# First projection reordered around its input loads, with six small moves in the second half of a two-layer decoder kernel

## The chip, the cores and the metric

One Trainium2 chip; the program runs on one of its cores. The metric is the device time of one execution in microseconds (us), the median of several runs. The core has a matrix engine (TensorE, PE in the profile, with its weight loads listed as PEld), a vector engine (VectorE, DVE), an activation engine (ScalarE, ACT), a general engine (GpSimd, POOL) and a queue engine that mostly issues DMA transfers (SyncE, SP). POOL can issue DMA transfers too. Each engine runs its own instructions strictly in the order in which they stand, and waits on semaphores where it needs another engine's or a transfer's result.

## The reference, cut to what matters

A trunk of two layers over 512 tokens of width 1024, all in float32. Layer 0 has dilated window attention, layer 1 attention with a forget gate over shared keys and values ("FoX"); each layer ends in a gated feed-forward part with a causal convolution of width 3.

```python
def dilated_mixer(xn, w_qkv, w_o, cos, sin):
    qkv = xn @ w_qkv                       # first projection: (512, 1024) x (1024, 2304)
    ...
def fox_mixer(xn, w_q, w_o, k, v, c):
    q = (xn @ w_q).reshape(B, T, B_HEADS, HEAD_DIM)
    for i in range(T // BLK):              # blocks of 128 queries, causal key prefixes
        s = einsum('bqhd,bkhd->bhqk', q_i, k[:, :q1]) * scale + (c_q - c_k)
        p = softmax(where(causal, s, NEG))
        outs.append(einsum('bhqk,bkhd->bqhd', p, v[:, :q1]))
    return concat(outs) @ w_o              # output projection: (512, 1024) x (1024, 1024)
def conv_ffn(xn, w_up, cw, cb, w_down):
    a = conv3(xn @ w_up) + cb
    gate, val = split(a, 2)
    return (gelu(gate) * val) @ w_down     # (512, 2816) x (2816, 1024)
def reference(...):
    for l in range(2):
        h = h + rms_norm(mix_l(rms_norm(h, g[0])), g[1])
        h = h + rms_norm(conv_ffn(rms_norm(h, g[2]), ...), g[3])
```

## The kernel before, in words

**Numbers.** Each float32 operand is cut into a high part in a shorter format and the rest, the low part; a product is then three matmuls: high by high, low by high, high by low. For weights, `Weights.high` (L55) makes the high part on ACT (L60), and `Weights.low` (L65) the low part on DVE (L69). A weight piece is 512 KB, named `wraw` (`wearly` for the first six) until it is cut, and `w` after that. `Weights.load` (L47) issues the transfers on SP's queue. `W.get()` hands out the next piece and cuts ahead as far as `W.ahead` says.

**Order.** The kernel is recorded with its own order (L221): instructions stand on each engine as the Python code emits them. Buffers come from pools (16 of 8 KB a partition, `t8`; 10 of 4 KB, `t4`; 8 of 2 KB, `t2`; 8 PSUM banks), and an instruction that takes a buffer waits until its last user has finished.

**First projection (L1251 to L1339).** The input x is loaded in half blocks: block b of 128 tokens, half i of 512 columns, `load_x(b, i)`, 256 KB each, from SP (L228). `transpose0` (L1257) turns four 128x128 squares of a half block on PE into PSUM (`xt_ps`), `split0` (L1266) makes the scaled high part on ACT (`xah`, L1271) and the low part on DVE (`xal`, L1273). `qk0(b, s)` (L1279) multiplies block b with weight piece s: two column groups k, three matmuls each, six matmuls of 128x512 (L1290) into `qk_ps`, which accumulates over four pieces. Before all this PE runs matmuls on a zeroed tile (`warm_up`, L243; `WARM = 4, 5`): four ahead of the first transposes, five behind them. The first real work needs the gains (`g0_rows`), half block (0, 0) and piece 0.

**FoX (L1840 to L1901).** A loop over m = 0 to 17; each m below 16 is a pair (j, i0) with j a pair of heads and i0 = 0 or 2, for two query blocks i0 and i0 + 1. In step m PE makes the scores of pair m (`s_ps`, L1759), the value products of pair m - 2 (`o_ps`, L1806), and then, in two half steps a = 0 and 1, a quarter of the next query projection (`q_ps`) and the transposes of the probabilities of pair m - 1 (`pT_ps`, L1791). POOL makes the bias one step ahead (L1740, L1741), DVE the maximum and the sum with the bias (`nm`, L1767), ACT the exponential (L1769), DVE the reciprocal and the scaling (L1777, L1779), ACT the copies of transposed probabilities (`pT`, L1793). From half step 26 on (`FILL`, m = 13) the first products of the output projection fill PE (`acc`, L277 to L279, with activations `OTb`); their weight pieces 1 to 3 are cut by `W.high()` from (j, i) = (6, 1) and `W.low()` from (6, 2) on. Piece 0 is cut earlier with an adding transfer.

**Sums of down weights.** The second-layer down projection uses sums of quarter blocks of its weights, made ahead and stored in the DRAM tile `dT`. `down_sums` (L590) is a generator that loads a pair of rows from SP, makes four DVE operations, and stores on a given queue. Inside the FoX loop `sums_between` (L1822) does the same for j = 2, 3, 4, 5: load on POOL's queue (L1827 to L1829), two DVE operations (L1831, L1832), two more (L1834, L1835), one store on POOL's queue (L1837). The table at L1854 says in which (m, half step) each part runs: with m = 2, 6, 10, 14 they are (m, 1), (m+1, 2), (m+2, 0), (m+2, 1), where half step 2 is the end of the step.

Of the kernel before, what the change touches and what calls it, by code (L numbers as in the profile page):

```python
# [9 lines left out]
F32 = mybir.dt.float32  # L10
# [8 lines left out]
KD = D // 128  # L19
# [3 lines left out]
EPS = 1e-6  # L23
# [5 lines left out]
ND = NF // 2  # L29
HALVES = (slice(0, 1024),), (slice(0, 512), slice(512, 1024))  # L30
WARM = 4, 5
LAST = 3
# [73 lines left out]
def trunk_kernel(ctx, tc, x, norm_gains, w_qkv_a, w_o_a, w_q_b, w_o_b, kv_norm, w_kvf, b_f,  # L106
# [127 lines left out]

    eps_t = cst.tile([128, 1], F32, name="eps_t")
    dve.memset(eps_t, EPS)
    g_rows = t2([8, 128], name="g0_rows")

    zero = t2([128, 512], BF16, name="zero")
    dve.memset(zero, 0.0)  # L240
    warm = bank([128, 512], name="warm")

# [347 lines left out]
    def down_sums(pairs, place, queue, lag, behind):  # L590
# [3 lines left out]
        for i in range(n + lag + behind):  # L594
# [15 lines left out]
            if i >= 0:  # L610
                l, j = pairs[i]
                for q, t in enumerate(live[i]):
                    queue.dma_start(dT[l][j, :, q * 1024:q * 1024 + 1024], t)
            yield
# [15 lines left out]
    def ffn(l, bd, cp, nxt, ahead):  # L630
# [343 lines left out]
        for c in range(2, NF):  # L974
            if c == NF - 4:
                pair_load(0)
            if c == NF - 3:
                sums = down_sums([(l, ND - 1), (1, 8 + l)], in_one, pool, 1, 0)
                next(sums)
# [277 lines left out]
    def transpose0(b, i):  # L1257
        n = 2 if (b, i) == (0, 0) else 4
        for k0 in range(0, 4, n):
            pt = bank([128, n, 128], name="xt_ps")  # L1260
            for k in range(n):
                c = (4 * i + k0 + k) * 128
                pe.transpose(pt[:, k, :], h[:, b, c:c + 128], ident)
                x_ps[b, 4 * i + k0 + k] = pt[:, k, :]
# [13 lines left out]

    def qk0(b, *pieces):  # L1279
        if b not in qk_banks:  # L1280
            qk_banks[b] = bank([128, T], name="qk_ps")
        o = qk_banks[b]
        for s in pieces:
            if s not in ws:
                ws[s] = [t.rearrange("p (k c) -> p k c", k=2) for t in W.get()]
            wh, wl = ws[s]
            for x, w in ((0, wh), (1, wh), (0, wl)):
                for k in range(2):
                    kc = 2 * s + k
                    pe.matmul(o, ax(0, b, kc)[x], w[:, k, :], start=kc == 0 and x == 0 and w is wh,  # L1290
                              stop=kc == KD - 1 and w is wl)

# [17 lines left out]
    qk0(2, 0, 1)  # L1310
    W.split(4)
# [27 lines left out]
    qk_post(0, 3, qk_banks[3])  # L1339
    sums = down_sums([(1, 6), (1, 7)], in_two, sp, 1, 3)  # L1340
    next(sums)
# [29 lines left out]

    down0 = down_sums([(0, j) for j in range(10)], in_one, sp, 1, 1)
    v_proj0([[L(qk_transpose, 0, 0), L(qk_transpose, 0, 1)],
# [448 lines left out]
    def sums_between(l, j):  # L1822
# [7 lines left out]
        yield  # L1830
        dve.tensor_tensor(a[:, 0:512], a[:, 512:1024], a[:, 0:512], ALU.subtract)  # L1831
        dve.tensor_tensor(a[:, 512:1024], b[:, 0:512], a[:, 512:1024], ALU.subtract)  # L1832
        yield
# [20 lines left out]
    for j, m in ((2, 2), (3, 6), (4, 10), (5, 14)):  # L1854
        g = sums_between(1, j)
        for i in ((m, 1), (m + 1, 2), (m + 2, 0), (m + 2, 1)):
            sums[i] = g
    for m in range(M + 2):
# [17 lines left out]
        for a in range(2):  # L1876
# [76 lines left out]
```

## Time and profile before

| what | us |
|---|---|
| median of 3 runs | 1107.63 (1106.81 to 1109.08) |
| the profiled execution's own time | 1107.05 |
| its span, first to last instruction | 1105.0 |
| PE busy | 1096.0 |
| DVE busy | 894.8 |
| ACT busy | 667.4 |
| POOL busy | 222.7 |

The profile lists for each instruction its start, its duration, and, in brackets, how long its engine stood idle before it and what ended that. The time line merges equal instructions that follow each other (x5 is five of them, with the time from the first start to the last end). Ends of matmuls are modelled and overlap the next start, so the pace of PE is read from start to start. Times in the text are counted from the start of the span. The profiled execution took 0.6 us less than the median.

### The profile page before, as it was taken

What the parts mean: (1) busy time and instruction counts of PE and PEld (TensorE: products, weight loads), DVE (VectorE), ACT (ScalarE), POOL (GpSimd) and SP (SyncE); (2) the same over time, 40 slices, a digit from 0 to 9 for tenths busy, and PEclk for the clock granted to TensorE, in tenths of its full rate; (3) what the DMA queues carried; (4) which work ended last, traced back from release to release, by engine and by line L of the source; (5) the groups of instructions that cost most, each with busy time, mean ns of one, the idle gap of its engine ahead of it and who ended that gap; (6) DMA issues with size and microseconds to landing.
All of it is one profiled execution on the core that took longest, in us unless ns stands there. A gap on an engine that the chain in (4) does not pass through costs nothing.

```text
span 1105.0 us, 18176 instructions
## 1 busy us (share of the span) xinstructions
PE 1096.0 (99%) x6608; PEld 948.5 (86%) x6608; DVE 894.8 (81%) x1510; ACT 667.4 (60%) x1120; POOL 222.7 (20%) x331
## 2 busy tenths in 40 slices
PE   9999999999999999999999999999999999999997
PEld 7988889899999988888888778789899999988886
DVE  5677778878887799997877877958978887799994
ACT  6654565656556547576565677655656566547572
POOL 4632101111111111000010766501111111111000
PEclk9999999999999999999999999999999999999999
DMA  9589854468788989894872677574468788999872
GB/s 320 109 290 407 335 151 136 112 148 191 180 194 206 278 312 341 284 321 98 210 153 77 209 229 204 160 233 134 106 146 192 176 200 210 265 314 342 292 248 77
DMA packets 185218, 237.33 MB, mean 215 GB/s; under 512 B 11872, under 2 KB 131672, under 8 KB 184616
## 3 DMA queue, kind: packets, MB, share of 16 engines
q1 hardware_dynamic: 167560, 176.61, 49.9%
q0 software_dynamic: 17568, 59.55, 23.2%
q8 instruction: 52, 0.85, 0.3%
q14 instruction: 38, 0.31, 0.1%
HBM read 170.28 MB, written 39.63 MB: 190 GB/s over the span
## 4 chain that ended last, share of the span: by engine, by line
PE 96%; ACT 2%; DVE 1%; issue 0%; DMA 0%; DVEq 0%; SPq 0%; ACTq 0%
PE up L277 13%; PE up L278 13%; PE up L279 13%; PE acc L277 8%; PE acc L278 8%; PE acc L279 8%; PE qk_ps L1290 2%; PE v_ps L277 2%; PE v_ps L278 2%; PE v_ps L279 2%; PE s_ps L1759 1%; PE o_ps L1806 1%; PE q_ps L277 1%; PE first L279 1%; PE first L277 1%; PE first L278 1%
## 5 line engine op out<-in xcount | busy, mean ns | idle before, releaser
L277 PE MATMUL acc<-w 128*128 128x512 f32 (+1 forms) x311 | 120.5, 388 | 0.0
L279 PE MATMUL acc<-w 128*128 128x512 f32 (+1 forms) x311 | 120.4, 387 | 0.0
L60 ACT CAST w<-wraw 128x1024 fp32r<-128x1024 f32 x96 | 99.0, 1049 | 9.6 <-issue 3.8
L278 PE MATMUL acc<-w 128*128 128x512 f32 (+1 forms) x267 | 103.2, 387 | 0.0
L639 ACT ACTIVATE bb<-up,conv 128x512 f32<-128x512 f32 x80 | 60.0, 776 | 67.3 <-DVE up L1020 42.8
L69 DVE TENSOR_TENSOR w<-wraw,w 128x1024 fp32r<-128x1024 f32 x66 | 88.0, 1353 | 12.9 <-ACT w L60 12.5
L278 PE MATMUL up<-xcl,w 128*128 128x512 f32 (+1 forms) x280 | 96.3, 344 | 0.0
L278 PE MATMUL up<-xbl,w 128*128 128x512 f32 (+1 forms) x280 | 96.3, 344 | 0.0
L277 PE MATMUL up<-xbh,w 128*128 128x512 f32 (+1 forms) x280 | 96.3, 344 | 0.0
L277 PE MATMUL up<-xch,w 128*128 128x512 f32 (+1 forms) x280 | 96.3, 344 | 0.0
L279 PE MATMUL up<-xbh,w 128*128 128x512 f32 (+1 forms) x280 | 96.2, 344 | 0.0
L279 PE MATMUL up<-xch,w 128*128 128x512 f32 (+1 forms) x280 | 96.2, 344 | 0.0
L277 PE MATMUL up<-xsh,w 128*128 128x256 f32 x320 | 90.6, 283 | 0.0
L278 PE MATMUL up<-xsl,w 128*128 128x256 f32 x320 | 90.6, 283 | 0.0
L279 PE MATMUL up<-xsh,w 128*128 128x256 f32 x320 | 90.6, 283 | 0.0
L279 PEld LDWEIGHTS acc<-w 128*128 128x128 f32 x311 | 58.4, 188 | 12.0
L277 PEld LDWEIGHTS acc<-w 128*128 128x128 f32 x311 | 58.4, 188 | 11.7
L642 DVE SCALAR_TENSOR_TENSOR bb<-up,conv,bb 128x510 f32<-128x510 f32 x80 | 59.9, 749 | 2.8
L640 DVE SCALAR_TENSOR_TENSOR bb<-up,conv,bb 128x511 f32<-128x511 f32 x80 | 59.4, 743 | 2.6 <-ACT bb L639 2.6
L277 PEld LDWEIGHTS up<-xsh,w 128*128 128x128 f32 x320 | 61.4, 192 | 0.0
L278 PEld LDWEIGHTS up<-xsl,w 128*128 128x128 f32 x320 | 61.4, 192 | 0.0
L279 PEld LDWEIGHTS up<-xsh,w 128*128 128x128 f32 x320 | 61.4, 192 | 0.0
(336 smaller groups left out, 3157.4 us busy)
## 6 DMA issues: line engine op xcount, KB each, us to landing
wraw<-in_w_up_dram SPq DMA_DIRECT2D x88, 512.0 KB
w<-wraw POOLq DMA_DIRECT2D x50, 512.0 KB, 5.9
dT<-dsums SPq DMA_DIRECT2D x24, 512.0 KB
hD<-hc POOLq DMA_DIRECT2D x44, 256.0 KB, 7.8
dact<-hD SPq DMA_DIRECT2D x44, 256.0 KB
wraw<-dT SPq DMA_DIRECT2D x22, 512.0 KB
wraw<-in_w_down_dram SPq DMA_DIRECT2D x22, 512.0 KB
dsums<-in_w_down_dram SPq DMA_DIRECT2D x18, 512.0 KB
```

What stands on the lines that cost most here:

```text
L60: self.nc.scalar.copy(pair[:, 0, s], raw[:, s])
L69: self.nc.vector.tensor_tensor(pair[:, 1, s], raw[:, s], pair[:, 0, s].bitcast(F32), ALU.subtract)
L277: pe.matmul(o, ah, bh, start=first, stop=False, skip_group_check=shared)
L278: pe.matmul(o, ah, bl, start=False, stop=False, skip_group_check=shared)
L279: pe.matmul(o, al, bh, start=False, stop=last, skip_group_check=shared)
L639: act.activation(bb[:, s, :], ps, AF.Identity, bias=cp[:, 3, ch:ch + 1], scale=cp[:, 2, ch:ch + 1])
L640: dve.scalar_tensor_tensor(bb[:, s, 1:], ps[:, :T - 1], cp[:, 1, ch:ch + 1], bb[:, s, 1:], ALU.mult, ALU.add)
L642: dve.scalar_tensor_tensor(bb[:, s, 2:], ps[:, :T - 2], cp[:, 0, ch:ch + 1], bb[:, s, 2:], ALU.mult, ALU.add)
L1290: pe.matmul(o, ax(0, b, kc)[x], w[:, k, :], start=kc == 0 and x == 0 and w is wh, stop=kc == KD - 1 and w is wl)
L1759: pe.matmul(s[i][hh][:, :nn], q[a][rows, qs], k[b][rows, :nn], start=n == 0, stop=n == 2)
L1806: pe.matmul(o[64 * hh:64 * hh + 64, i * 128:(i + 1) * 128], Vt[hd // 8][:, k, (hd % 8) * 64:(hd % 8) * 64 + 64], pT[j, i, hh][:, k, :], st ...
```

## The change

Line numbers behind the first edits shift by one to six; the new kernel's rows below carry its own.

- **Loads.** Piece 1 of the weights is asked for behind half blocks (1, 0) and (2, 0), not ahead of them.
- **Warm-up.** Six matmuls ahead of the first transposes and three behind them (before four and five). The zeroed tile is set ahead of the epsilon constant.
- **First projection.** `qk0` takes its matmuls in another order (high, low, high, low for the two column groups with the weight's high part, then the two with its low part) and can call a function in their midst, between the first group's and the second's. The transposes of half blocks (1, 0), (2, 0), (3, 0) go there, and the products of pieces 0 and 1 come in the order 0 for blocks 0, 1, 2, then 1 for blocks 0, 1, 2. The first-half transposes of all blocks use two PSUM banks of two squares each, and are split two at a time.
- **Stores.** `down_sums` takes a list of queues; the second store of `down1` goes to SP and not to POOL.
- **Sums.** `sums_between` has five parts: the first of its DVE operations runs half a step earlier, in (m+1, 1).
- **Output weights.** `W.high()` from (6, 0) and `W.low()` from (6, 1), half a step earlier each.

```diff
-WARM = 4, 5
+WARM = 6, 3
...
-    W.load(2)
+    W.load(1)
     load_x(1, 0)
     load_x(2, 0)
+    W.load(2)
     load_x(3, 0)
...
-                    queue.dma_start(dT[l][j, :, q * 1024:q * 1024 + 1024], t)
+                    queue[min(i, len(queue) - 1)].dma_start(dT[l][j, :, q * 1024:q * 1024 + 1024], t)
...
     def transpose0(b, i):
-        n = 2 if (b, i) == (0, 0) else 4
+        n = 4 if i else 2
...
-    def qk0(b, *pieces):
+    def qk0(b, *pieces, between=None):
...
-            for x, w in ((0, wh), (1, wh), (0, wl)):
-                for k in range(2):
-                    kc = 2 * s + k
-                    pe.matmul(o, ax(0, b, kc)[x], w[:, k, :], start=kc == 0 and x == 0 and w is wh,
-                              stop=kc == KD - 1 and w is wl)
+            for x, w, k in ((0, wh, 0), (1, wh, 0), (0, wh, 1), (1, wh, 1), (0, wl, 0), (0, wl, 1)):
+                kc = 2 * s + k
+                if w is wh and x == 0 and k and between is not None:
+                    between()
+                pe.matmul(o, ax(0, b, kc)[x], w[:, k, :], start=kc == 0 and x == 0 and w is wh,
+                          stop=kc == KD - 1 and w is wl)
...
     W.split(1)
+    qk0(0, 0, between=L(transpose0, 1, 0))
+    split0(1, 0, (0, 1))
     split0(0, 0, (2, 3))
+    qk0(1, 0, between=L(transpose0, 2, 0))
+    split0(2, 0, (0, 1))
     W.split(2)
-    qk0(0, 0)
-    x0(1, 0)
-    qk0(0, 1)
-    x0(2, 0)
-    qk0(1, 0)
+    split0(1, 0, (2, 3))
+    qk0(2, 0)
+    qk0(0, 1, between=L(transpose0, 3, 0))
+    split0(2, 0, (2, 3))
+    split0(3, 0)
+    qk0(1, 1)
     W.split(3)
-    qk0(1, 1)
-    x0(3, 0)
-    qk0(2, 0, 1)
+    qk0(2, 1)
     W.split(4)
...
-    down1 = down_sums([(1, j) for j in range(2)], in_two, pool, 1, 1)
+    down1 = down_sums([(1, j) for j in range(2)], in_two, [pool, sp], 1, 1)
...
         dve.tensor_tensor(a[:, 0:512], a[:, 512:1024], a[:, 0:512], ALU.subtract)
+        yield
         dve.tensor_tensor(a[:, 512:1024], b[:, 0:512], a[:, 512:1024], ALU.subtract)
...
-        for i in ((m, 1), (m + 1, 2), (m + 2, 0), (m + 2, 1)):
+        for i in ((m, 1), (m + 1, 1), (m + 1, 2), (m + 2, 0), (m + 2, 1)):
             sums[i] = g
...
-            if live and (j, i) >= (6, 2):
+            if live and (j, i) >= (6, 1):
                 W.low()
-            if live and (j, i) >= (6, 1) and W.n_split < wo + 4:
+            if live and (j, i) >= (6, 0) and W.n_split < wo + 4:
                 W.high()
```

**PE in the first projection.** The rows from the first product on, before (`w_160` is piece 0, `w_169` piece 1, `h_79` the input, `qk_ps_174` block 0's sums):

```order
L1290 MATMUL qk_ps_174<-w_160,xah0_133 128x512 x2
L1290 MATMUL qk_ps_174<-w_160,xal0_135 128x512 x2
L1290 MATMUL qk_ps_174<-w_160,xah0_133 128x512 x2
L1263 MATMUL xt_ps_181<-ident_109,h_79 128x128 x4
L1290 MATMUL qk_ps_174<-w_169,xah0_133 128x512 x2
L1290 MATMUL qk_ps_174<-w_169,xal0_135 128x512 x2
```

and in the changed kernel (`w_160` is piece 0, `qk_ps_165` and `qk_ps_186` are the sums of blocks 0 and 1):

```order
L1292 MATMUL qk_ps_165<-w_160,xah0_135 128x512
L1292 MATMUL qk_ps_165<-w_160,xal0_137 128x512
L1264 MATMUL xt_ps_168<-ident_109,h_79 128x128 x2
L1264 MATMUL xt_ps_171<-ident_109,h_79 128x128 x2
L1292 MATMUL qk_ps_165<-w_160,xah0_135 128x512
L1292 MATMUL qk_ps_165<-w_160,xal0_137 128x512
L1292 MATMUL qk_ps_165<-w_160,xah0_135 128x512 x2
L1292 MATMUL qk_ps_186<-w_160,xah0_135 128x512
```

The transposes of half block (1, 0) now come behind two products, not six, and the next products are block 1's with piece 0 in place of block 0's with piece 1.

**DVE around the sums, step m = 3 of FoX.** Before, from the scaling of (1, 2) on (`rl` and `bias` are the softmax, `OTb0` the low part of the attention output):

```order
L1779 TENSOR_SCALAR bias_6332<-bias_6332,rl_6460 128x384 x2
L1777 RECIPROCAL rl_6481<-ls_6440 128x2
L1779 TENSOR_SCALAR bias_6362<-bias_6362,rl_6481 128x512 x2
L1820 TENSOR_TENSOR OTb0_6446<-o_ps_6313,OTb0_6446 128x512
L1831 TENSOR_TENSOR dsums_6375<-dsums_6375 128x512
L1832 TENSOR_TENSOR dsums_6375<-dsums_6375 128x512
```

and in the changed kernel:

```order
L1784 TENSOR_SCALAR bias_6335<-bias_6335,rl_6463 128x384 x2
L1836 TENSOR_TENSOR dsums_6378<-dsums_6378 128x512
L1782 RECIPROCAL rl_6485<-ls_6443 128x2
L1784 TENSOR_SCALAR bias_6365<-bias_6365,rl_6485 128x512 x2
L1825 TENSOR_TENSOR OTb0_6449<-o_ps_6316,OTb0_6449 128x512
L1838 TENSOR_TENSOR dsums_6378<-dsums_6378 128x512
```

The first operation on the sums stands ahead of the second scaling; the same happens in m = 7, 11 and 15.

**ACT around the output weights, end of step m = 12.** Before (`wraw_7180` is output weight piece 1):

```order
L1793 COPY pT_7332<-pT_ps_7331 128x384
L1793 COPY pT_7338<-pT_ps_7337 128x384
L1793 COPY pT_7355<-pT_ps_7354 128x512
L1793 COPY pT_7362<-pT_ps_7361 128x512
L60 CAST w_7370<-wraw_7180 128x1024
L1769 ACTIVATE bias_7312,ls_7404<-bias_7312,nm_7403 128x384 x2
```

and in the changed kernel (`wraw_7183` is piece 1, `wraw_7346` piece 2):

```order
L1798 COPY pT_7335<-pT_ps_7334 128x384
L1798 COPY pT_7341<-pT_ps_7340 128x384
L60 CAST w_7348<-wraw_7183 128x1024
L1798 COPY pT_7362<-pT_ps_7361 128x512
L1798 COPY pT_7369<-pT_ps_7368 128x512
L60 CAST w_7378<-wraw_7346 128x1024
L1774 ACTIVATE bias_7315,ls_7412<-bias_7315,nm_7411 128x384 x2
```

Piece 1's cut stands between the copies of two probability blocks, and piece 2's ahead of the next exponentials.

More of the change, by code (lines that the diff above doesn't have):

```diff
@@ L29 @@
 ND = NF // 2
-HALVES = (slice(0, 1024),), (slice(0, 512), slice(512, 1024))
-WARM = 4, 5
+WARM = 6, 3
+HALVES = [(slice(0, 1024),), (slice(0, 512), slice(512, 1024))]
 LAST = 3
@@ L233, in load_gain @@
         return t
-    eps_t = cst.tile([128, 1], F32, name="eps_t")
-    dve.memset(eps_t, EPS)
     g_rows = t2([8, 128], name="g0_rows")
@@ L240, in trunk_kernel @@
     dve.memset(zero, 0.0)
+    eps_t = cst.tile([128, 1], F32, name="eps_t")
+    dve.memset(eps_t, EPS)
     warm = bank([128, 512], name="warm")
@@ L977, in ffn @@
             if c == NF - 3:
-                sums = down_sums([(l, ND - 1), (1, 8 + l)], in_one, pool, 1, 0)
+                sums = down_sums([(l, ND - 1), (1, 8 + l)], in_one, [pool], 1, 0)
                 next(sums)
@@ L1339, in trunk_kernel @@
     qk_post(0, 3, qk_banks[3])
-    sums = down_sums([(1, 6), (1, 7)], in_two, sp, 1, 3)
+    sums = down_sums([(1, 6), (1, 7)], in_two, [sp], 1, 3)
     next(sums)
@@ L1370, in v_post @@
         dve.tensor_scalar(V[2][:, b, :], o[:, 256:512], scale_of(1, b), None, ALU.mult)
-    down0 = down_sums([(0, j) for j in range(10)], in_one, sp, 1, 1)
+    down0 = down_sums([(0, j) for j in range(10)], in_one, [sp], 1, 1)
     v_proj0([[L(qk_transpose, 0, 0), L(qk_transpose, 0, 1)],
```

## The prediction

> **What bounds the kernel now.** I read the busy shares first, then the chain of waits by engine, then what PE waited for, and only then the time lines of the two places that the change touches.
>
> ```profile
> PE 1096.0 (99%) x6608; PEld 948.5 (86%) x6608; DVE 894.8 (81%) x1510; ACT 667.4 (60%) x1120; POOL 222.7 (20%) x331
> ...
> PE 96%; ACT 2%; DVE 1%; issue 0%; DMA 0%; DVEq 0%; SPq 0%; ACTq 0%
> ...
> PE warm L245 <- DVE zero L240: 1.2, 1, 1.2
> PE acc L278 <- DVE w L69: 0.8, 1, 0.8
> PE g_ps L267 <- DMA g_rows<-in_norm_gains_dram: 0.5, 1, 0.5
> ```
>
> PE bounds everything: it is busy for 1096.0 of 1105.0 us, and its named waits are three, 2.5 us in sum. The change removes no matmul. So only four things can pay: PE's waits, a faster pace of its first matmuls, an earlier start of real work, and short holes between matmuls that the modelled ends hide. The time line of PE at the start:
>
> ```profile
> 1.23 1.89 PE L245 MATMUL warm<-zero 128*128 128x512 bf16 x4 [1.23 <-DVE zero L240]
> 3.65 0.24 PE L267 MATMUL g_ps<-ident,g_rows 8*128 8x8 f32 x1 [0.53 <-DMA g_rows<-in_norm_gains_dram]
> 3.82 1.12 PE L1263 MATMUL xt_ps<-ident,h 128*128 128x128 f32 x4
> 4.73 2.34 PE L245 MATMUL warm<-zero 128*128 128x512 bf16 x5
> 8.57 1.05 PE L1290 MATMUL qk_ps<-w,xah 128*128 128x512 f32 x2
> 9.43 0.72 PE L1263 MATMUL xt_ps<-ident,h 128*128 128x128 f32 x4
> 10.45 0.63 PE L1290 MATMUL qk_ps<-w,xal 128*128 128x512 f32 x2
> 10.92 0.62 PE L1290 MATMUL qk_ps<-w,xah 128*128 128x512 f32 x2
> 33.30 0.28 PE L277 MATMUL v_ps<-w,xah 128*128 128x256 f32 x1
> ```
>
> Read from start to start, two 128x512 products take 0.86 us at 8.57 and 0.47 at 10.45: 0.43 and 0.23 each. PE works at half pace until about 9.65, and from then on at full pace. The warm matmuls run at 0.43 too (five from 4.73 end at 6.87, where the first product begins). From the transposes at 9.43 to the next stage at 33.30 PE has no hole.
>
> **The first projection.** What PE waits for there:
>
> ```profile
> 3.58 1.42 SPq L228 DMA_DIRECT2D h<-in_x_dram  x3
> 5.06 1.35 ACT L60 CAST w<-wearly 128x512 fp32r<-128x512 f32 x2
> 7.83 1.28 ACT L60 CAST w<-wearly 128x512 fp32r<-128x512 f32 x2 [0.90 <-DMA wearly<-in_w_qkv_a_dram]
> 9.18 0.73 PEld L1263 LDWEIGHTS xt_ps<-ident,h 128*128 128x128 f32 x4 [0.27 <-DMA h<-in_x_dram]
> ```
>
> *Start.* Six warm matmuls end at 1.23 + 6 x 0.43 = 3.8, when the gains are there (3.65), so the 0.53 us wait is filled, and the transposes start about 0.1 later than before. Behind them come three warm matmuls, not five: the first product starts at 4.8 + 3 x 0.43 = 6.1, not 6.87. It finds its operands (piece 0's first cast, from 5.06, is done by 5.74). The two products then end by 6.9.
>
> *Loads.* Now PE wants half block (1, 0), which takes the place that piece 1's first transfer had in SP's queue; before, the three half blocks were issued from 3.58, behind piece 1. Piece 1's first transfer was waited for until 7.83, the upper bound. The two 256 KB transfers behind it landed in 9.18 - 7.83 = 1.35, 0.68 each; piece 0 was there by 5.74, so the lower bound is 6.4. I take 7.5, near the upper end, since place and bytes are those of the row at 7.83. PE waits 0.6 us there. Piece 1 goes to where (1, 0) and (2, 0) stood, 9.2 and 9.9; ACT cuts it from 10.5, behind the splits of (2, 0), and PE needs it after 18 products and two sets of transposes, near 12.2. That order of casts costs nothing while this cover of 1 us holds.
>
> *Rest of the stage.* In the trace PE needs 33.30 - 9.43 = 23.9 us from these transposes on, with six products behind it. In the new order two are behind it, so four more at 0.23 are ahead: 24.8. From 7.5 this ends at 32.3, a gain of 1.0. The new order inside `qk0` and the two-bank transposes add no instruction on PE; ACT and DVE have the same work in another order, with the idle time above. From both sides: data at 6.4 lets PE go on at 6.9, a gain of 1.6; data at 7.83, a gain of 0.7.
>
> *Pace.* This sum takes full pace from 7.5 on. In the trace full pace began 6.0 us after PE last stood idle (3.65 to 9.65). With the wait filled, the unbroken stretch begins at 1.2, and the same 6.0 us end at 7.2, ahead of 7.5. If the pace still changes at 9.65, the 2.15 us from 7.5 do 46% less work: 1.0 us back, and the gain is nil. If it changes at 5, the data still set the time; the bound is 1.6.
>
> [...]
>
> I book **-1.0 us** (0 to -1.6).
>
> **Output weights and sums in FoX.** PE's rows in four steps with i0 = 2 (m = 5, 9, 11, 13) and at the products of weight piece 1:
>
> ```profile
> 644.89 1.99 PE L1759 MATMUL s_ps<-kst,qst 64*128 64x384 f32 x12
> 646.81 1.75 PE L1806 MATMUL o_ps<-pT,Vt 128*64 128x128 f32 x28
> ...
> 671.26 1.97 PE L1759 MATMUL s_ps<-kst,qst 64*128 64x384 f32 x12
> 673.16 1.75 PE L1806 MATMUL o_ps<-pT,Vt 128*64 128x128 f32 x28
> ...
> 684.68 1.49 PE L1759 MATMUL s_ps<-kst,qst 64*128 64x384 f32 x12
> 686.09 1.75 PE L1806 MATMUL o_ps<-pT,Vt 128*64 128x128 f32 x28
> ...
> 696.23 1.84 PE L1759 MATMUL s_ps<-kst,qst 64*128 64x384 f32 x12
> 698.00 1.75 PE L1806 MATMUL o_ps<-pT,Vt 128*64 128x128 f32 x28
> ...
> 701.70 0.47 PE L277 MATMUL acc<-w,OTb 128*128 128x512 f32 x1
> 702.95 0.50 PE L278 MATMUL acc<-w,OTb 128*128 128x512 f32 x1 [0.77 <-DVE w L69]
> ```
>
> The scores take 1.41 at 684.68 where no sums run, but 1.92, 1.90 and 1.77 one step after sums: holes of 0.5, 0.5 and 0.36 that the list of waits does not show. The step from 701.70 to 702.95 is 1.25 where 0.32 is usual after transposes: 0.93 lost. What DVE, ACT and POOL do around them:
>
> ```profile
> 618.89 1.12 POOL L613 DMA_DIRECT2D dT<-dsums  x2
> 631.92 0.58 POOL L1827 DMA_DIRECT2D dsums<-in_w_down_dram  x1
> ...
> DMA to landing us min/median/max: 6.6/6.6/6.6
> ...
> 636.01 0.85 DVE L1779 TENSOR_SCALAR bias<-bias,rl 128x384 f32<-128x384 f32 x2
> 639.05 0.85 DVE L1831 TENSOR_TENSOR dsums<-dsums 128x512 f32<-128x512 f32 x1
> 663.65 0.17 DVE L1777 RECIPROCAL rl<-ls 128x2 f32<-128x2 f32 x1 [0.36 <-ACT bias L1769]
> 671.53 0.68 DVE L1567 TENSOR_TENSOR qst<-q_ps,qst 128x512 fp32r<-128x512 f32 x1
> 697.91 1.07 ACT L60 CAST w<-wraw 128x1024 fp32r<-128x1024 f32 x1
> 701.68 1.22 DVE L69 TENSOR_TENSOR w<-wraw,w 128x1024 fp32r<-128x1024 f32 x1
> ```
>
> *Piece 1.* Its low part runs from 701.68 to 702.9 and PE waits for it. Half a step earlier it stands ahead of DVE's last `qst` and is done near 699: **-0.93**. DVE is then 1.2 us later with the next maxima, and the other low parts move up as well; PE needs those a step later, and step 13's value products (1.75 at 698.00) and first output products lie between, which hides it; without them up to 1.2 would show.
>
> *ACT.* The cast (1.07) now stands between the copies of two probability blocks, which PE multiplies from 698.00 on. They were done at 697.9, and the second pair is now done at 698.9; its products are the last 16 of the 28 and start about 0.7 behind 698.00. That leaves a hole of 0.2 to 0.5 in place of the 0.36 at 696.23: **+0.1**.
>
> *Sums.* The first operation (0.85) fills the 0.36 that DVE idles before 663.65, so DVE's chain to `qst` (671.53), which ends the hole at 671.26, comes 0.36 earlier: **-0.4** in m = 9. In m = 3 the load is late: issued at 631.92, landed 6.6 later at 638.5, while DVE is ready at 636.9. DVE would stand 1.6 us, of which its own 0.36 of idle time is free: it is late by up to 1.3 (the 0.85 is spent here and saved at 639.05), and the hole at 644.89 grows by that. The store that leaves POOL frees 1.12 us at 618.89, which moves POOL's next steps and so the load earlier, by at most that. Bounds: -0.4 to +1.3; I take **+0.4**. On SP the two stores stand between two key loads that have several steps of slack: 0.
>
> The sum for FoX is -0.93 + 0.1 - 0.4 + 0.4 = **-0.8** (-1.6 to +0.2).
>
> **Sum.** -1.0 - 0.8 = -1.8 against the profiled execution's own 1107.05 gives 1105.25; the median shown is 0.6 above that execution, so the same from the median gives 1105.8. I take **1105.3**, nearer the execution whose rows give the terms and which lies within the runs' range.
>
> **Rivals.**
>
> *Both places pay in full* (15%): data at 6.4 and no late load, -1.6 - 1.6 = -3.2: 1103.9. For it: POOL's freed 1.12 us. Against it: the row at 7.83.
>
> *The pace changes no earlier* (18%): nil in the first projection, -0.8 in FoX: 1106.3. For it speaks that nothing in the trace shows what sets the moment.
>
> *DVE stands for the sums' load in m = 3* (14%): +1.3 in place of +0.4: total -0.9, 1106.2.
>
> *Slower: the wait for half block (1, 0) breaks the busy stretch* (10%). If full pace needs 6.0 us counted from the end of PE's last idle time, it comes at 7.5 + 6.0 = 13.5. Of 6.0 us at half pace 46% are lost, 2.8, against the 1.0 gained: +1.8, and with FoX's -0.8 the kernel is 1.0 slower: 1108.1. It decides as soon as PE stands for the load for longer than the trace's 0.53. Against it: the stretch from 1.2 would have ended first.
>
> [...]
>
> *The change does not move what it says* (3%): the second transposes or casts are held by a bank or buffer; 1107.3.
>
> **Chances and range.** My forecast has 40% (1104.5 to 1106.1). A difference below 0.2%, 2.2 us, cannot be told from none here, so faster means under 1105.4 from the median of 1107.6. A little over half of my forecast's 40%, all of the 15%, and some of the others (the better ends of their bounds) lie there: 0.46. Slower, above 1109.8, needs the slower rival with other losses: 0.09. The rest, 0.45, is within 0.2%. With the rivals on both sides the range is 1103.0 to 1108.0.
>
> **What would show it.** The last product before the stage at L277 ends near 32.3 and not 33.3; the transposes of (1, 0) have a wait on their load of about 0.6; two products at 8 to 9 us stand 0.47 apart, not 0.86; PE has no wait on a weight's low part near 702; the scores in m = 9 take 1.5, in m = 5 more than 1.9; DVE waits for the sums' load in m = 3. I am wrong if the pace changes at 9 or later, if PE stands over 1 us for the load, or if a new wait of PE over 0.5 us stands elsewhere in FoX.

## The result, and the profile after

The changed kernel takes 1104.54 us (median of 8 runs, 1104.09 to 1104.94), the kernel before 1107.51 on the same chip (8 runs, 1106.80 to 1109.08): 2.97 us less, ratio 0.9974 with a 95% interval of 0.9963 to 0.9984. The forecast was 1105.3, a gain of 1.8. The profiled execution took 1104.09 with a span of 1102.3, against 1107.05 and 1105.0.

The page of the changed kernel, its span, busy times and the chain of waits by engine:

```profile
span 1102.3 us, 18174 instructions
...
PE 1093.3 (99%) x6608; PEld 947.3 (86%) x6608; DVE 895.4 (81%) x1510; ACT 666.4 (60%) x1120; POOL 224.8 (20%) x329
...
PE 97%; ACT 1%; DVE 1%; DMA 0%; issue 0%; SPq 0%; DVEq 0%; ACTq 0%
```

Nothing changed in kind. PE still bounds the kernel, with the same 6608 matmuls, and its busy time fell by 2.7 us, as much as the span: what was saved was pace and holes that the modelled ends hide. What PE waits for by name:

```profile
PE warm L245 <- DVE eps_t L240: 1.2, 1, 1.2
PE o_ps L1811 <- ACT pT L1798: 0.6, 1, 0.6
PE xt_ps L1264 <- DMA h<-in_x_dram: 0.4, 1, 0.4
PE qk_ps L1292 <- ACT w L60: 0.3, 1, 0.3
```

The waits for the gains (0.5) and for DVE's low part of a weight (0.8) are gone. Three others stand in their place, and the 0.6 us on ACT's copy `pT` lies in FoX, where none was forecast. PE's time line at the start:

```profile
1.20 2.74 PE L245 MATMUL warm<-zero 128*128 128x512 bf16 x6 [1.20 <-DVE eps_t L240]
...
4.88 0.81 PE L245 MATMUL warm<-zero 128*128 128x512 bf16 x3
5.98 0.50 PE L1292 MATMUL qk_ps<-w,xah 128*128 128x512 f32 x1 [0.29 <-ACT w L60]
6.32 0.40 PE L1292 MATMUL qk_ps<-w,xal 128*128 128x512 f32 x1
7.11 0.66 PE L1264 MATMUL xt_ps<-ident,h 128*128 128x128 f32 x4 [0.40 <-DMA h<-in_x_dram]
...
8.07 0.86 PE L1292 MATMUL qk_ps<-w,xah 128*128 128x512 f32 x3
8.77 0.40 PE L1292 MATMUL qk_ps<-w,xal 128*128 128x512 f32 x1
...
31.84 0.28 PE L278 MATMUL v_ps<-w,xah 128*128 128x256 f32 x1
```

The first product of the kernel before stood here:

```profile
6.51 1.42 PE L1290 MATMUL qk_ps<-w,xah 128*128 128x512 f32 x2
```

Now it starts at 5.98. From 8.07 three products take 0.70 to the next row, 0.23 each, which is full pace, where before two took 0.86. The half block (1, 0) is waited for until 7.11, and the next stage begins at 31.84, 1.45 earlier. The FoX steps that the prediction showed, in the changed kernel (the same matmuls, lines shifted by five):

```profile
643.14 1.58 PE L1764 MATMUL s_ps<-kst,qst 64*128 64x384 f32 x12
644.65 1.75 PE L1811 MATMUL o_ps<-pT,Vt 128*64 128x128 f32 x28
...
669.10 1.65 PE L1764 MATMUL s_ps<-kst,qst 64*128 64x384 f32 x12
670.68 1.75 PE L1811 MATMUL o_ps<-pT,Vt 128*64 128x128 f32 x28
...
693.75 1.49 PE L1764 MATMUL s_ps<-kst,qst 64*128 64x384 f32 x12
695.17 1.87 PE L1811 MATMUL o_ps<-pT,Vt 128*64 128x128 f32 x28
...
699.31 0.39 PE L279 MATMUL acc<-w,OTb 128*128 128x512 f32 x1
...
702.51 0.66 PE L1811 MATMUL o_ps<-pT,Vt 128*64 128x128 f32 x8 [0.61 <-ACT pT L1798]
...
705.20 1.33 PE L1796 MATMUL pT_ps<-ident,bias 128*128 128x128 f32 x8
```

Read each row against the row of before with the same work. The scores of m = 5 begin 1.75 earlier (644.89 to 643.14), what follows them 2.16 (646.81 to 644.65): the hole in them closed by 0.41. In m = 9 it is 0.32 (2.16 to 2.48), in m = 13 0.35 (2.48 to 2.83). The second product with weight piece 1 is 3.64 earlier (702.95 to 699.31). Then 0.67 is given back in front of 702.51 and 0.34 within the eight transposes from 705.20 on, which take 1.33 where 1.03 is usual. In the kernel before PE did the same work without a hole:

```profile
705.20 0.88 PE L1806 MATMUL o_ps<-pT,Vt 128*64 128x128 f32 x12
...
708.11 1.03 PE L1791 MATMUL pT_ps<-ident,bias 128*128 128x128 f32 x8
```

The last matmul of the kernel ends up 2.61 earlier.

| where the time went | forecast | profiled execution |
|---|---|---|
| first projection, to the stage at 31.84 | -1.0 | -1.45 |
| from there to the scores of m = 5 | 0 | -0.30 |
| scores of m = 5 | +0.4 | -0.41 |
| scores of m = 9 | -0.4 | -0.32 |
| scores of m = 13 and the value products behind them | +0.1 | -0.24 |
| wait for the low part of piece 1 | -0.93 | -0.92 |
| new holes behind it (702.51, 705.9) | 0 | +1.01 |
| sum to the last matmul | -1.8 | -2.6 |

From the last matmul to the end of the span 0.13 more are saved, and outside the span 0.22. Of the -0.30, 0.21 lie in the query products just ahead of the scores of m = 3: before, PE's weight load stood 0.4 us there for an adding transfer (`w<-wraw`), now it does not. The other 0.09 lie ahead of FoX, where traces of the same code differ by up to 0.17. So the time came out 0.8 us below the forecast, but two lines of FoX have the wrong sign, and the largest new loss was booked at nothing. The experiments ask three things: what sets the start, what closed the hole ahead of m = 3 and the one in m = 5, and why the gain at piece 1 was given back.

### The profile page after: what moved, and what is told of

It is laid out like the page before. It is cut to its first block, busy times and chain, and to the rows that moved or that the text cites. A ratio compares the mean times of both kernels' runs of the same rounds, so it can differ in the third digit from the quotient of the medians.

```text
span 1102.3 us, 18174 instructions
## 1 busy us (share of the span) xinstructions
PE 1093.3 (99%) x6608; PEld 947.3 (86%) x6608; DVE 895.4 (81%) x1510; ACT 666.4 (60%) x1120; POOL 224.8 (20%) x329
## 4 chain that ended last, share of the span: by engine, by line
PE 97%; ACT 1%; DVE 1%; DMA 0%; issue 0%; SPq 0%; DVEq 0%; ACTq 0%
PE up L278 13%; PE up L279 13%; PE up L280 13%; PE acc L278 8%; PE acc L280 8%; PE acc L279 8%; PE v_ps L278 2%; PE v_ps L279 2%; PE v_ps L280 2%; PE qk_ps L1292 2%; PE o_ps L1811 2%; PE s_ps L1764 2%; PE q_ps L278 2%; PE pT_ps L1796 2%; PE first L280 1%; PE first L278 1%
```

## The experiments

Each was timed against the kernel before in the same comparison; "median" is the difference to it there. With an interval of about 0.1% on each side (1 us), the places are judged by the trace, one for each kernel, and places of under about 0.1 us say nothing.

### Each half alone

The edits of the first projection alone (this diff is against the changed kernel), and the rest alone:

```diff
-    down1 = down_sums([(1, j) for j in range(2)], in_two, [pool, sp], 1, 1)
+    down1 = down_sums([(1, j) for j in range(2)], in_two, pool, 1, 1)
...
-        for i in ((m, 1), (m + 1, 1), (m + 1, 2), (m + 2, 0), (m + 2, 1)):
+        for i in ((m, 1), (m + 1, 2), (m + 2, 0), (m + 2, 1)):
...
-            if live and (j, i) >= (6, 1):
+            if live and (j, i) >= (6, 2):
                 W.low()
-            if live and (j, i) >= (6, 0) and W.n_split < wo + 4:
+            if live and (j, i) >= (6, 1) and W.n_split < wo + 4:
```

> Only the edits of the first projection (loads, warm-up, order in qk0), FoX as before. In the changed kernel the stage at L277 begins 1.45 us earlier than before (31.84, not 33.30). Theory: that is the whole of the start's part and is carried through; 33.30 becomes 31.8 to 31.9, and the span is 1.45 below the kernel before (1103.5), the FoX holes (0.93 at weight piece 1, 0.4 to 0.5 in the scores of m = 5, 9, 13) all there. Rival: the start shifts the loads behind it and FoX's holes change with it; the span then gains 1.0 or less, or 2.0 and more.

Measured: 1106.38, median -0.86 (ratio 0.9994, 0.9985 to 1.0003). The stage began at 32.92, not 31.84, though the code of the start is the same. The second half was as before, with its wait of 0.8 on the weight. So 1.45 came from the two executions that were compared and is not the start's worth; neither theory allowed for that. The wait on the half block's load was 1.0 us here, in the changed kernel's own trace 0.4.

> Only the edits of the second half (store on SP, five parts of the sums, output weights half a step earlier), first projection as before. Theory: -1.2 in all (-0.3 in m = 3, -0.4 in m = 5, -0.33 in m = 9, -0.36 in m = 13, -0.8 at weight piece 1, +0.67 at the value products behind it and +0.34 at the transposes): span 1103.8. Rival: a part of this comes from the start's shift against the transfers; then fewer than three of the four score holes close and the gain is under 0.6.

This kernel is the one before with the `+` and `-` of the diff above exchanged. Measured: 1105.44, median -1.80 (0.9985, 0.9976 to 0.9994). From its stage on (33.00, against 33.30 in the profiled execution before) the trace gains 0.99 to the last matmul, with the same steps as the changed kernel: closed holes in m = 5, 9 and 13, 0.9 at piece 1 and the same give-back behind it. The halves add up within the interval, -0.86 and -1.80 against -2.97 together, and more than half comes from FoX, where 0.8 was forecast.

### What sets the start

```diff
-    W.load(1)
+    W.load(2)
     load_x(1, 0)
     load_x(2, 0)
-    W.load(2)
```

> The changed kernel with weight piece 1 asked for ahead of half blocks (1, 0) and (2, 0), as before. In five traces of the kernels so far with the new order the stage at L277 begins 24.7 us after the transposes of (1, 0) start, whatever the pace did earlier. Theory: the landing of (1, 0) sets the stage; it comes near 9.2 as in the old order, PE stands about 2.5 us for it, the next stage begins at 33.9, later than before the change (33.3): +2 against the changed kernel, 1106.5. Rival: the warm-up and the pace made the gain; the stage begins by 32.7, under +0.9.

Measured: 1107.40, median +0.40 (1.0005, 0.9996 to 1.0015), runs from 1105.67 to 1112.15. Rows of PE's time line, and of the view by windows (length; busy time and instructions of PE, PEld, DVE, ACT and POOL; granted clock, DMA share and rate):

```profile
8.83 1.12 PE L1263 MATMUL xt_ps<-ident,h 128*128 128x128 f32 x4 [2.12 <-DMA h<-in_x_dram]
...
35.01 0.28 PE L277 MATMUL v_ps<-w,xah 128*128 128x256 f32 x1
```

```profile
5.10:8.60 3.50, 1.51 (x6) 0.42 (x4) 1.81 (x4) 1.34 (x4) 0.00 (x0) 1.00 0.95 299
8.60:12.00 3.40, 3.17 (x10) 2.69 (x11) 1.13 (x4) 1.14 (x4) 0.00 (x0) 0.50 1.08 379
```

PE stands 2.12 us for the half block, near what was expected, but the stage begins at 35.01 and not 24.7 behind the landing (33.55). The second view shows why: PE had run at full pace, was busy for only 1.51 of the 3.5 us in which most of the stand fell, and then got half its clock for the next 3.4. From the transposes at 8.83 to the next stage it took 26.2 us, where every undisturbed execution took 24.7.

```diff
-WARM = 6, 3
+WARM = 4, 5
```

> The changed kernel with four warm matmuls ahead of the first transposes and five behind. Theory (the landing of (1, 0) sets the stage): PE waits 0.5 for the gains again, starts its first product at 6.5 instead of 5.98 and ends both products between 7.0 and 7.6, about when (1, 0) lands; the stage begins at 31.7 to 32.9 as in the kernels with 6 and 3, and the median is within 0.4 of the changed kernel. Rival: the filled wait and the earlier first product are worth their 0.5 to 0.9, and the pace changes later since the busy stretch is broken at 3.6: over 0.6 slower, two products still 0.86 apart after 8.5.

Measured: 1105.32, median -1.68 (0.9985, 0.9976 to 0.9994), 0.8 above the changed kernel's median. The rival held in part. The wait for the gains is back (0.5), the pace changed at 8.72, and PE began the transposes of (1, 0) at 7.96. But the half block's last part landed at 7.91 here, so that with full pace too PE could not have begun them earlier. The stage began at 33.04, 0.79 behind the mean of the new start (table below): 0.42 of it is this late landing, and 0.38 is the half pace behind it, 25.09 us to the stage and not 24.7.

The warm-up alone on the kernel before (`WARM = 6, 3` and the zeroed tile first):

> The kernel before with the warm-up of the change alone (six and three matmuls, the zeroed tile first). [...] Rival: the first product's 0.9 us is carried through, 0.9 faster.

Measured: 1107.11, median -0.12 (0.9998, 0.9989 to 1.0006). PE is early and stands for the load:

```profile
9.02 0.66 PE L1263 MATMUL xt_ps<-ident,h 128*128 128x128 f32 x4 [0.94 <-DMA h<-in_x_dram]
```

The stage began at 32.82. So the warm-up is worth nothing that the times show without the loads, and the loads lose 0.4 us in the trace without the warm-up: the start is the later of a landing and a pace, and the change moves both. From all traces of this study (the clock by the trace's record of what was granted):

| executions | full pace from | transposes of (1, 0) | wait before them | next stage | from one to the other |
|---|---|---|---|---|---|
| old start (before, `fox_only`) | 9.67, 6.95 | 9.43, 9.20 | 0, 0.70 | 33.30, 33.00 | 23.87, 23.80 |
| `warm_only` | 5.11 | 9.02 | 0.94 | 32.82 | 23.80 |
| new start, nine executions | 4.56 to 7.22 | 7.04 to 8.21, mean 7.54 | 0 to 1.35 | 31.71 to 32.92, mean 32.25 | 24.67 to 24.74 |
| `old_warm` | 8.72 | 7.96 | 0 | 33.04 | 25.09 |
| `old_loads` | 5.16, half again 8.58 to 11.99 | 8.83 | 2.12 | 35.01 | 26.17 |

In the nine the last column is constant to 0.07 while the start of the transposes varies by 1.2. In eight of them PE stands for half block (1, 0) and begins 0.04 to 0.05 us after its last part has landed (7.07 to 8.16): there the landing alone sets the stage. In the ninth (`old_weights`) it had landed at 6.77, and PE came at 7.04, since its two products ran at half pace until 6.95.

### What closed the hole ahead of m = 3 and the one in m = 5

```diff
-    down1 = down_sums([(1, j) for j in range(2)], in_two, [pool, sp], 1, 1)
+    down1 = down_sums([(1, j) for j in range(2)], in_two, [pool], 1, 1)
```

> The changed kernel with the second store of down1 back on POOL's queue. In the changed kernel POOL issues the load of the first sums at 628.97 and it lands 3.9 us later, 2.1 before DVE's first sum at 635.04; before it was issued at 631.92 (1.4 later against the steps) and took 6.6. Theory: the store on POOL delays that load, both its issue and its landing; it then lands about 2 us after DVE is ready, DVE stands 1.5 to 2.2 for it in m = 3, the hole in the scores of m = 5 comes back to 0.5 to 1.5 and the span grows by 0.6 to 1.5. Rival: the long landing has another cause (loads on SP); DVE does not wait and the span stays within 0.2.

Measured: 1106.28, median -0.72 (0.9994, 0.9985 to 1.0003), 1.7 above the changed kernel's median: more than half of the change's gain is gone with one store. Its rows, POOL's first and then DVE's and PE's, from their time lines; the fourth is the answer on the load's line:

```profile
617.84 1.12 POOL L614 DMA_DIRECT2D dT<-dsums  x2
628.92 1.53 POOL L1745 TENSOR_SCALAR bias<-ck,cq 128x512 f32<-128x512 f32 x2 [0.68 <-DMA w<-wraw]
630.88 0.58 POOL L1832 DMA_DIRECT2D dsums<-in_w_down_dram  x1
DMA to landing us min/median/max: 6.3/6.3/6.3
637.23 0.77 DVE L1836 TENSOR_TENSOR dsums<-dsums 128x512 f32<-128x512 f32 x1 [1.44 <-DMA dsums<-in_w_down_dram]
645.43 0.96 PE L1764 MATMUL s_ps<-kst,qst 64*128 64x512 f32 x5 [0.62 <-DVE qst L1572]
```

The same in the changed kernel, where the store is SP's:

```profile
613.34 1.91 SPq L614 DMA_DIRECT2D dT<-dsums  x2
628.97 0.59 POOL L1832 DMA_DIRECT2D dsums<-in_w_down_dram  x1
DMA to landing us min/median/max: 3.9/3.9/3.9
635.04 0.88 DVE L1836 TENSOR_TENSOR dsums<-dsums 128x512 f32<-128x512 f32 x1
```

On SP the store leaves 4.1 us earlier against the step's own start (the stages lie 0.39 apart in the two traces). On POOL the adding transfer behind it is issued 0.6 later against the step (622.59, with the store on SP 621.58), POOL stands 0.68 for that, and the load of the sums is issued 1.5 us later and lands 6.3 after its issue instead of 3.9. DVE, which now wants it half a step earlier, stands 1.44 us, and PE then stands for `qst`: against the changed kernel 1.0 us is lost in m = 5 and 0.16 ahead of m = 3, where PE's weight load stands for the adding transfer again (0.3). The other 0.1 of the 1.24 to the last matmul lies ahead of FoX. DVE's wait is the one that the prediction placed in the changed kernel. It is real (m = 5 is 0.6 slower than before the change), and the store that moved prevents it. All traces agree: the load landed 3.8 to 4.0 us after its issue in the ten with the store on SP, and 6.0 to 6.6 in the four with it on POOL; PE's weight load stood for the adding transfer in those four (0.2 to 0.4) and in none of the ten. Why a load that is issued 1.5 later also takes 2.4 longer to land is not shown. The time outside the span was 0.2 longer here (2.0 against 1.8), as in the kernel before; what that is stays open, for it came back in a later kernel with the store on SP (`early_sums`, 2.0).

```diff
-        for i in ((m, 1), (m + 1, 1), (m + 1, 2), (m + 2, 0), (m + 2, 1)):
+        for i in ((m, 1), (m + 1, 2), (m + 2, 0), (m + 2, 1)):
```

> The changed kernel with the sums in four parts, the first two operations together at (m + 1, 2). Theory: the half step earlier is what closes the holes in the scores; they come back in m = 5, 9 and 13 (0.4, 0.33, 0.36), the span grows by 0.7 to 1.1. Rival: the holes close because the store left POOL; then m = 5 stays closed and the loss is 0.3 to 0.7 with m = 9 and 13 alone, or nothing.

(The `yield` between the first two sums goes with it.) Measured: 1105.57, median -1.43 (0.9987, 0.9978 to 0.9996). Against the changed kernel the trace loses 0.08 in m = 5, 0.33 in m = 9, 0.35 in m = 13 and 0.22 in the value products behind it, and wins 0.30 back from 702 on; with 0.09 ahead of FoX it is 0.77 in all to the last matmul. The scores of m = 9 and 13 take 1.97 and 1.84 again, those of m = 5 1.66. So the half step closes m = 9 and 13, and the store closes the hole ahead of m = 3 and most of m = 5: each theory is right for its own steps. In m = 5 the two edits hang together. From their first matmul to the first value product behind them, its scores take 1.92 us with neither edit, 1.59 with the store alone, 2.52 with the half step alone and 1.51 with both.

### Why the gain at piece 1 was given back

```diff
-            if live and (j, i) >= (6, 1):
+            if live and (j, i) >= (6, 2):
                 W.low()
-            if live and (j, i) >= (6, 0) and W.n_split < wo + 4:
+            if live and (j, i) >= (6, 1) and W.n_split < wo + 4:
```

> The changed kernel with W.high and W.low at their old half steps. Theory: the earlier weights took away 0.8 to 0.93 at piece 1 and gave nearly all of it back, 0.67 at the value products (ACT's third cast stands ahead of a pT copy) and 0.34 at the transposes; so the wait on DVE's low part (0.8) is back, the wait on ACT's pT (0.6) is gone, and the span is within 0.3 of the changed kernel's 1102.3. Rival (as predicted): the earlier weights are worth 0.8, the wait on pT has another cause and stays; 1103.1 or more.

Measured: 1104.36, median -2.88 (0.9975, 0.9965 to 0.9985). The wait on DVE's low part is back (0.8), the wait on `pT` is gone, and from the stage to the last matmul this kernel gains 1.13, the changed kernel 1.16. So the weights half a step earlier are worth nothing: 0.03 us is less than traces of the same code differ by. In the changed kernel's ACT the cast of piece 3 stands ahead of the copy that the eight value products at 702.51 need:

```profile
700.66 0.37 ACT L1798 COPY pT<-pT_ps 128x256 f32<-128x256 f32 x1
700.93 1.05 ACT L60 CAST w<-wraw 128x1024 fp32r<-128x1024 f32 x1
701.88 0.58 ACT L1798 COPY pT<-pT_ps 128x512 f32<-128x512 f32 x1
```

Before, a cast (of piece 2) stood there too (702.59, the copy behind it 703.54), but the products came at 705.20, since PE had just stood 0.93 us for DVE. The next kernel puts that cast behind the copy:

```diff
+            if live and (j, i) == (6, 3):
+                W.high()
             if live and (j, i) >= (6, 1):
                 W.low()
-            if live and (j, i) >= (6, 0) and W.n_split < wo + 4:
+            if live and (j, i) in ((6, 0), (6, 1)):
                 W.high()
```

> The changed kernel with the third cast of the output weights on ACT half a step later, behind the pT copy and just ahead of its low part on DVE. Theory: the cast ahead of the copy is what PE stands 0.6 us for; the wait on pT goes, the low part of piece 3 is still in time, and the span falls by 0.3 to 0.67 to 1101.6 to 1102.0. Rival: DVE is as late as ACT there (its chain has no idle time from 697 to 706); the wait goes but the transposes behind it stand longer, and the gain is under 0.15. Third: the low part comes too late and PE waits for DVE w: no gain or a loss up to 0.5.

Measured: 1104.75, median -2.49 (0.9978, 0.9969 to 0.9986); from the stage on 0.16 worse than the changed kernel. The wait on `pT` is gone, and 3.6 us later PE stands for DVE:

```profile
701.96 0.88 PE L1811 MATMUL o_ps<-pT,Vt 128*64 128x128 f32 x12
...
705.55 0.66 PE L1796 MATMUL pT_ps<-ident,bias 128*128 128x128 f32 x4 [0.54 <-DVE OTb L1825]
706.40 0.63 PE L1796 MATMUL pT_ps<-ident,bias 128*128 128x128 f32 x4 [0.20 <-DVE nm L1772]
```

The second answer held: DVE is as late as ACT. Two kernels take work off DVE there. The first lets an adding transfer make the low part of piece 2, with the late cast:

```diff
+            if live and (j, i) == (6, 3):
+                W.high()
             if live and (j, i) >= (6, 1):
                 W.low()
-            if live and (j, i) >= (6, 0) and W.n_split < wo + 4:
+            if live and (j, i) == (6, 0):
                 W.high()
+            if live and (j, i) == (6, 1):
+                W.high_added()
```

> The changed kernel with the low part of output weight piece 2 made by an adding transfer (one more ACT operation of 1.06 us, none on DVE: 1.21 us less at 700.27), and the third cast behind the pT copy. Theory: from 695 to 706 DVE's chain sets the time, whatever PE names as waited for; with 1.21 us less on it both holes of the changed kernel (0.67 at the value products, 0.34 at the transposes) go, and from 697 to the end 0.6 to 1.0 is gained. Rival: ACT or the adding transfer (5.6 us to landing, needed near 703.5) is next; PE waits for that instead, and the gain is under 0.3.

Measured: 1106.23, median -1.00 (0.9990, 0.9981 to 0.9999). The rival held: POOL issued the transfer at 698.55, 3.35 us after it was free, since it waited for ACT, and the landing was 7.8 us behind that:

```profile
706.36 0.50 PE L279 MATMUL acc<-w,OTb 128*128 128x512 f32 x1 [2.54 <-DMA w<-wraw]
```

The second takes the late cast, and starts the sums of j = 4 a step earlier, so that 3.9 us of DVE's work leave the stretch from 687 to 694:

```diff
-    for j, m in ((2, 2), (3, 6), (4, 10), (5, 14)):
+    for j, m in ((2, 2), (3, 6), (4, 9), (5, 14)):
```

> The kernel with the late third cast, and the sums of j = 4 one step earlier (m = 9 in the table and not 10): 3.9 us of DVE's work leave the stretch from 687 to 694 and go to the step before, in which DVE is busy for 3.87 of 7 us. With the late cast alone the wait on pT went, but the transposes behind it stood 0.6 longer. Theory: DVE's chain from 687 to 706 sets both; with it earlier no hole of over 0.3 is left between 697 and 710, and from 697 to the end 0.6 to 1.0 is gained against the changed kernel, so the median is 1103.6 to 1104.1. Rival: the hole at the transposes has another cause (a bank, or ACT's copies) and stays; gain under 0.2. Third: the sums open a hole of 0.3 to 0.5 in the scores of m = 11, which takes half of the gain.

Measured: 1104.66, median -2.34 (0.9979, 0.9969 to 0.9988), in the trace 0.13 worse than the changed kernel from the stage on. In m = 11 a hole opened that had not been there, since DVE stood for the sums' load, which landed 5.4 us after its issue. The rows are DVE's and PE's in m = 11, then DVE's and PE's further on:

```profile
681.77 0.69 DVE L1836 TENSOR_TENSOR dsums<-dsums 128x512 f32<-128x512 f32 x1 [2.27 <-DMA dsums<-in_w_down_dram]
683.85 0.96 PE L1764 MATMUL s_ps<-kst,qst 64*128 64x512 f32 x5 [0.24 <-DVE qst L1572]
...
695.78 1.23 DVE L69 TENSOR_TENSOR w<-wraw,w 128x1024 fp32r<-128x1024 f32 x1 [0.96 <-ACT w L60]
...
706.28 0.63 PE L1796 MATMUL pT_ps<-ident,bias 128*128 128x128 f32 x4 [0.20 <-DVE nm L1772]
```

The hole costs 0.75: the third answer, at a higher price than expected. Behind it the kernel is 0.74 faster than the changed kernel to the last matmul, with no wait at the value products. That looks like the theory's gain and is not one. DVE was free earlier, as intended, but then stood 0.96 us for ACT's cast, and from there on its rows lie within 0.15 us of `late_cast` (the low part of piece 2 at 700.62, there at 700.76). PE came later by the hole, and so its waits behind it were shorter; the transposes ran at 706.28, in `late_cast` at 706.40. So in these two traces PE's own arrival did not set the time there, but ACT's cast and DVE's chain behind it. Whether DVE's freed time would pay without the hole in m = 11 stays open.

### A loose end

```diff
-        pool.dma_start(dT[l][j].rearrange("p (q d) -> p q d", q=2), t)
+        sp.dma_start(dT[l][j].rearrange("p (q d) -> p q d", q=2), t)
```

> The changed kernel with the four 1 MB stores of the sums on SP's queue as well. In every run so far the time outside the span is 2.0 us with the second store of down1 on POOL and 1.8 with it on SP. Theory: each POOL transfer costs some time outside the span; four fewer instructions give 1.7 or less. Rival: it is not the number of POOL transfers; 1.8 stays. Inside the span: SP's loads behind the stores have slack, within 0.2 of the changed kernel; if they have none, PE waits for a key or weight load and it is slower by 0.5 or more.

Measured: 1104.91, median -2.32 (0.9979, 0.9970 to 0.9988), outside the span still 1.8: the rival held. In the trace 0.52 was lost from the stage on, 0.4 of it in a wait for a small load behind SP's queue (`cv_rows`) near 723.

No experiment beat the changed kernel by more than its interval.

## Why the prediction was right and where it was wrong

**First projection: right, in its steps and its size.** First product at 6.1: 5.98 in eight of nine executions, 5.95 in one. (That the old one started at 6.87 was misread, it was 6.51; the sum did not use it.) Data at 7.5: the transposes began at 7.54 on the mean of nine. The rest 24.8: 24.67 to 24.74. Stage at 32.3: 32.25 on the mean. The gain against the old start (33.15, the mean of two) is 0.9, forecast 1.0, and the kernel with the start alone had a median 0.86 lower; the profiled execution's 1.45 is an early landing (7.07) against an old start whose pace changed late. The wait for the half block is 0.4 there and 0 to 1.35 elsewhere, against 0.6. Too narrow were the bounds of the landing: 7.83 as the upper end was passed twice (7.99, 8.16), since it was taken from one execution as if a load's landing were fixed.

**Pace: harmless here, but the step was wrong.** "In the trace full pace began 6.0 us after PE last stood idle" took one interval as a rule. The same start gave 9.67 and 6.95, so 6.0 and 3.25 us after the idle time. In the unbroken start it came at 4.56 to 7.22, that is 3.4 to 6.0 us after 1.2, always ahead of the transposes of (1, 0), which is why little hung on it (0.3 in `old_weights`). What sets the moment the traces do not show.

**The slower rival: a real loss, seen in one trace, with the wrong point.** It was to decide "as soon as PE stands for the load for longer than the trace's 0.53". Stands of 0.99 and 1.35 cost nothing beyond themselves; one of 2.12 cost 1.45 on top (26.17 against 24.72 from the transposes to the stage). The rival had counted 2.8 for it, about twice that: it took 6.0 us at half pace, where `old_loads` had 3.41.

**FoX, sums and store: this step failed.** The prediction wrote "In m = 3 the load is late: issued at 631.92, landed 6.6 later", and of the store that leaves POOL, that it "moves POOL's next steps and so the load earlier, by at most" 1.12; it took +0.4, and booked the store on SP at 0. It held the landing time fixed while moving the work that made it. With the store on SP the load is issued 1.5 earlier and lands in 3.9, so DVE has it 2 us before it is wanted. Up to m = 5 FoX gained 0.62 (0.21 and 0.41) where 0.4 of loss was booked, and the one edit that was to cost nothing is worth the most: 1.1 to 1.2 us on PE against `pool_store`, where the predicted wait appears, with 0.6 lost in m = 5 against the kernel before. The m = 9 term was right (-0.4, measured -0.32); m = 13, whose hole was to be replaced by another, closed by the same half step.

**Output weights: the first step right, the next late thing missed.** "-0.93" at piece 1 came as -0.92. The rule to say what is late next was followed for the first cast and for DVE's other low parts, not for the third cast (+0.67) nor for DVE's chain behind it (+0.34). "PE needs those a step later, and step 13's value products ... lie between, which hides it" looked at piece 2 and 3 as PE's operands, not at what the same engines must do for the softmax in between. Of the -0.8 booked here (-0.93 + 0.1) nothing was kept. The wait of 0.61 for `pT` is one of the signs that the prediction itself had named for being wrong: a new wait of PE over 0.5 us elsewhere in FoX.

**The sum.** The profiled execution gained 2.96 where 1.8 was forecast: 1.11 more from the stage to the end of the scores of m = 5, 0.45 more at the start, most of it an early landing, 0.34 more in m = 13, and 0.35 behind the last matmul and outside the span that was in no term, against 0.08 less in m = 9 and 1.01 of holes behind piece 1 that were in no term either. The gain was 1.6 times the forecast, and that it was not further off is luck: errors of opposite sign.

## What to carry to other kernels

Before a term is made from a transfer's landing time, ask which edit of the same change moves the traffic or the queue that made that time; a store booked at nothing on its new queue can be worth most on the queue that it left (here 1.1 to 1.2 us on PE). A wait that one engine causes can hide a like lateness of another (here 0.61 for ACT's `pT`, and in `late_cast`, without it, 0.54 for DVE's `OTb`): where a wait is removed, follow every engine of the step to the end of the next step, and expect nothing where a neighbour has no idle time. A stretch that runs faster behind a new hole may only be taking up that hole (0.74 behind 0.75 in `early_sums`), so compare where each engine stands on the clock, not the length of the stretch. A start that waits for loads can vary between executions of the same code (here the transposes of (1, 0) began at 7.04 to 8.21 in nine), so take its bounds from several, and judge it by what is constant (here the 24.67 to 24.74 us from those transposes to the stage).

## What the runs showed of the hardware that was not expected

The landing of half block (1, 0) was set by its last parts, and with the new start it scattered from 6.77 to 8.16 us in nine executions. In `start_only` 14 of its 16 parts were there by 6.66 us and the last at 8.16; in the changed kernel 13 by 6.36 and the last at 7.07. Half block (2, 0), behind it, was complete 0.63 and 0.64 us after those last parts. Why a part is late the traces do not show.

Full pace, once given, was lost in one trace though PE was not idle throughout. In `old_loads` PE was busy for 1.45 of the 3.42 us from 5.16 to 8.58, in which most of the stand of 2.12 fell, and got half its clock for the next 3.41. In `sp_stores` it was busy for 1.72 of the 3.4 us from 4.6 to 8.0, in which nearly all of its stand of 1.35 fell, and kept its pace. These are one execution each, and what made the difference is not shown.

Ahead of the first full pace PE was busy nearly without a break. In all 14 traces it was busy for 95% or more of the 3.41 us just ahead (the length of the half-paced stretch in `old_loads`). In the kernel before it was busy for 2.88 us from 2.84 to 6.25, where the wait of 0.53 for the gains fell, and for all 3.41 from 6.26 to 9.67, after which full pace began; in `old_warm` it was 2.88 and 3.33 in the two such stretches ahead of 8.72. In `fox_only`, with the same start code as the kernel before, the wait for the gains was 0.58 and ended at 3.70, PE was busy for 3.25 of the 3.41 us from 3.54 to 6.95, and full pace began at 6.95. So the same code, with nearly the same wait in its warm-up, got full pace 2.72 us apart in two executions. What sets the moment is not shown.
